# Splitting the last output pass of a two-layer diffusion step into two passes of 160 tokens

## The chip, the cores and the metric

The kernel runs on one core of one Trainium2 chip. The metric is the device time of one launch in microseconds (us). Five engines work side by side, each with its own instruction queue: TensorE (PE; its weight loads are listed apart as PEld), VectorE (DVE), ScalarE (ACT), GpSimd (POOL) and SyncE (SP), which starts the transfers to and from the device memory.

## The reference, cut to what matters

The program is one inference step of a two-layer backbone over 128 context tokens and 512 latent tokens, 640 in all, with 1024 features each. Each layer runs FFN, token mixer, FFN; after each of these six stages (numbered 0 to 5) comes a residual sum and a LayerNorm. The change lies in the last one, stage 5:

```python
def layer_norm(x, g, b):
    xf = x.astype(jnp.float32)
    mu = xf.mean(-1, keepdims=True)
    var = jnp.square(xf - mu).mean(-1, keepdims=True)
    return ((xf - mu) * lax.rsqrt(var + LN_EPS) * g + b).astype(x.dtype)

def swiglu(h, w_in, w_out):
    g, u = jnp.split(h @ w_in, 2, axis=-1)
    return (jax.nn.silu(g) * u) @ w_out
...
    x = layer_norm(ALPHA * x + 0.5 * g3 * swiglu(modulate(x, sh3, sc3), ffn_w_in_i[1], ffn_w_out_i[1]),
                   ln_g_i[2], ln_b_i[2])
```

The hidden width of the FFN is 2816. Everything is computed in float32.

## The kernel before

Features lie on the 128 partitions, tokens along the columns: `x` holds eight feature tiles (`dt` 0 to 7) of 640 tokens. The tokens are cut in two halves of 320 (`c` 0 and 1, `CSL`). A product of float32 numbers is made of three products of rounded parts (high times high, high times low, low times high); each is one matmul with a 128x128 weight tile that is loaded just for it. One such product of one hidden block, in `product`, is therefore three loads and three matmuls (lines 527, 528 and 529).

The 22 hidden blocks of the FFN come in four groups (`GROUPS`). For each group the hidden part is computed, and then the output products of that group are added to `x`. In the last group, of five blocks, one output tile is 15 matmuls (five blocks by three). `do_out(dt, c)` makes one output tile: it multiplies into one bank of PSUM and calls `residual`, in which DVE scales the bank by the gate, adds it to `x` (line 353), and GpSimd sums tiles 0 to 6 of `x` for the mean (line 357). All eight tiles of `c` = 0 run first, then all eight of `c` = 1. All weights of this last group stay in ten pairs of weight tiles, so that both halves use the same ones.

`norm_steps` is the LayerNorm of one half, a generator that is stepped by `tick` between the matmuls of other work:

- `mu`: two float32 products that give the mean in every partition (lines 401 and 403), copied by ACT to `mus` (line 405)
- `x - mu`: five tiles on DVE, three on GpSimd (line 411), squares on ACT (line 413)
- `va`: sums of the squares, with weights of only 32 columns (line 420)
- `rq`, `rx`: root on ACT (line 425), reciprocal on DVE (line 426), spread by a mask (line 428)
- `rs`: one product that copies the reciprocal root to every partition (line 432)
- `x * rs` on DVE (line 436), then, in stage 5, scale and shift on ACT (line 445) and one transfer of the tile to `y` from SP (line 447)

The LayerNorm of `c` = 0 is stepped between the output products of `c` = 1. The LayerNorm of `c` = 1 follows when all products are done; in stage 5 nothing is left that could run beside it. The program is written in this order, and a scheduler that walks through it fixes the order on each engine; after that each engine works strictly in its order.

Of the kernel before, what the change touches and what calls it, by code (L numbers as in the profile page):

```python
# [12 lines left out]
F32 = mybir.dt.float32  # L13
F32R = mybir.dt.float32r
AF = mybir.ActivationFunctionType
ALU = mybir.AluOpType
# [3 lines left out]
P = 128  # L20
D = 1024
KD = D // P
CTX = 128
LAT = 512
T = CTX + LAT
CH = T // 2
# [20 lines left out]
TICK_OUT = (1, 3, 4, 5)  # L47
TICK_IN = (1, 3, 4, 6)
# [26 lines left out]
XPOOL = ((), ())  # L75
XDVE = (tuple(range(8)), (2, 5))
MPOOL = (2, 5, 7)
LAG = 2
T1, T2, T4 = (0, 1), (2, 3), (4, 5)
GTYPE_P = (0, 1, 1, 0)  # L80
# [4 lines left out]
def kernel(  # L85
# [5 lines left out]
    te, act, dve, pool, sp = nc.tensor, nc.scalar, nc.vector, nc.gpsimd, nc.sync  # L91
# [16 lines left out]
    sm = ctx.enter_context(tc.tile_pool(name="sm", bufs=2))  # L108
# [4 lines left out]
    def tmp(name, cols=T, parts=P, dt=F32):  # L113
        t = tp.tile([P, UW], F32, tag="t", name=name)
        return t[:parts, :cols]
# [9 lines left out]
    mean_w = const.tile([P, P], F32, name="mean_w")  # L125
    dve.memset(mean_w, 1.0 / D)
    qmask = const.tile([P, 4], F32, name="qmask")
# [184 lines left out]
    x = res.tile([P, KD, T], F32, name="x")  # L312
# [20 lines left out]
        for _ in range(2 * n):  # L333
            fill_step()

    CSL = (slice(0, CH), slice(CH, T))
    SEG = (((slice(0, CTX), 1), (slice(CTX, CH), 0)), ((slice(CH, T), 0),))

    def gemm(ps, wh, wl, rows, cols, kh, kl):
        n = len(rows)  # L340
# [5 lines left out]
                tick()  # L346

    s1t = [res.tile([P, CH], F32, name=f"s1_{c}") for c in range(2)]

    def residual(ps, dt, c, st, nsum=0):  # L350
        for sl, z in SEG[c]:
# [41 lines left out]
        warm = sm.tile([P, 1], F32, tag="warm", name="warm")  # L393
        act.activation(warm, src[:, 0:1], AF.Sqrt, bias=eps_t, scale=0.0)

    QC = CH // 4

    def norm_steps(c, st, bank, nsum):
        sl = CSL[c]
        mu = bank(f"mu{st}_{c}")[:, :CH]  # L400
        pin(te.matmul(mu, mean_w, s1t[c], start=True, stop=(nsum == KD)))
        for dt in range(nsum, KD):
            te.matmul(mu, mean_w, x[:, dt, sl], start=False, stop=(dt == KD - 1))
        mus = tmp(f"mus{st}_{c}", CH)
        act.copy(mus, mu)
        va = None
        for half in range(2):
            sqs = []
            for dt in range(4 * half, 4 * half + 4):
                eng = pool if dt in MPOOL else dve  # L410
                eng.tensor_tensor(x[:, dt, sl], x[:, dt, sl], mus if eng is pool else mu, ALU.subtract)
                sq = tmp(f"sq{st}_{c}_{dt}", CH)
                act.activation(sq, x[:, dt, sl], AF.Square)
                sqs.append(sq)
            yield
            if va is None:
                va = bank(f"va{st}_{c}")[:, :QC]
            for i, sq in enumerate(sqs):
                for q in range(4):
                    ins = te.matmul(va[32 * q:32 * q + 32], mean_w[:, 0:32], sq[:, q * QC:(q + 1) * QC],  # L420
                                    start=(half == 0 and i == 0), stop=(half == 1 and i == 3))
                    if i == 0 and q == 0:
                        pin(ins)
        rq = sm.tile([P, QC], F32, tag="rq", name=f"rq{st}_{c}", bufs=1)
        act.activation(rq, va, AF.Sqrt, bias=eps_t)
        dve.reciprocal(rq, rq)
        rx = tmp(f"rx{st}_{c}", CH)
        dve.tensor_tensor(rx.rearrange("p (q n) -> p q n", q=4), rq.unsqueeze(1).broadcast_to([P, 4, QC]),
                          qmask.unsqueeze(2).broadcast_to([P, 4, QC]), ALU.mult)
        yield  # L430
        rs = bank(f"rs{st}_{c}")[:, :CH]
        pin(te.matmul(rs, mean_w, rx, start=True, stop=True))
        xms = []
        for dt in range(KD + (LAG if st < 5 else 0)):
            if dt < KD:
                ins = dve.tensor_tensor(x[:, dt, sl], x[:, dt, sl], rs, ALU.mult)
                if dt > LAG:
                    pin(ins)
            if st < 5:
                if dt < KD:  # L440
                    xms.append(modulate_in(dt, c, st + 1))
                if dt >= LAG:
                    modulate_out(dt - LAG, c, xms[dt - LAG])
            else:
                act.activation(x[:, dt, sl], x[:, dt, sl], AF.Identity, bias=lnb[:, st, dt:dt + 1],
                               scale=lng[:, st, dt:dt + 1])
                sp.dma_start(out=a["y"][:, dt, sl], in_=x[:, dt, sl])

    class LayerNorm:
# [3 lines left out]
        def tick(self):  # L453
            self.n += 1
            while self.ticks and self.n >= self.ticks[0]:
                self.ticks.pop(0)
                next(self.gen, None)
# [6 lines left out]
    pending = []  # L464
# [5 lines left out]
    def settle():  # L470
        while pending:
            pending.pop(0).finish()
# [81 lines left out]
    def ffn(l, j, hp, fbank, following):  # L554
        idx = 2 * l + (0 if j == 0 else 1)
        st = 3 * l + j
# [9 lines left out]
        for g0, g1 in GROUPS:  # L566
# [67 lines left out]
            last = g1 == NF  # L634
# [4 lines left out]
            def do_out(dt, c):  # L639
                while len(out_units) < -(-(nf * (dt + 1)) // 4):  # L640
                    o = len(out_units) * 512
                    n = min(1024, nf * D - o)
                    out_units.extend(uload(a["wout"][idx, :, g0 * D + o:g0 * D + o + n], n,
                                          pool if not last and len(out_units) // 2 % OPOOL else dve))
                b = fbank(f"o{idx}_{g0}_{dt}_{c}")
                product(b, out_units, nf * dt, [(hh[k][:, CSL[c]], hl[k][:, CSL[c]]) for k in range(nf)])
                residual(b, dt, c, st, nsum)

# [8 lines left out]
            for i in range(KD + skew):  # L657
                if i < KD:
                    do_out(i, 0)
                    if i < LLAST or not last:  # L660
                        for _ in range(LOUT[0]):
                            next(lanes, None)
                if i >= skew:
                    do_out(i - skew, 1)
                    if not last:
                        for _ in range(LOUT[1]):
                            next(lanes, None)
                if i == KD - 1 and last:
                    pending.append(LayerNorm(0, st, fbank, nsum, TICK_OUT))
                if i >= KD - 1 and last:  # L670
                    tick()
                while coming and i >= KD - 1 and len(out_units) - NUNIT <= ready and nf * (i - skew + 1) >= 4 * ready + 8:
                    key = coming.pop(0)
                    at["w"] = len(following) - len(coming) - 1
                    early[key] = wload(a[key[0]][key[1:]])
                    ready += 2
            if last:
                for _ in lanes:
                    pass
                assert not coming  # L680
                at["u"] = 6
                settle()
                pending.append(LayerNorm(1, st, md_bank if (st + 1) % 3 == 1 else fbank, nsum, TICK_IN))

    def project_load(name, i):
        return [u for h in range(2) for u in halves(wget((name, i, h)))]
# [1044 lines left out]
```

## Time and profile before

| | us |
|---|---|
| three runs | 2796.84, 2799.68, 2804.33 |
| median | 2799.68 |
| the profiled execution, whole | 2800.67 |
| its span in the trace | 2798.9 |
| PE busy over the span | 96% |
| granted TensorE clock, mean over the span | 0.985 of full |

The span begins with the first and ends with the last recorded instruction; the 1.8 us between it and the whole time lie outside the trace. Times of rows count from the start of the span. The stage that the change touches is the last 38.6 us of it, from 2760.28, where the first product of `c` = 1 starts, to 2798.9.

### The profile page before, as it was taken

What the parts mean: (1) busy time and instruction counts of PE and PEld (TensorE: products, weight loads), DVE (VectorE), ACT (ScalarE), POOL (GpSimd) and SP (SyncE); (2) the same over time, 40 slices, a digit from 0 to 9 for tenths busy, and PEclk for the clock granted to TensorE, in tenths of its full rate; (3) what the DMA queues carried; (4) which work ended last, traced back from release to release, by engine and by line L of the source; (5) the groups of instructions that cost most, each with busy time, mean ns of one, the idle gap of its engine ahead of it and who ended that gap; (6) DMA issues with size and microseconds to landing.
All of it is one profiled execution on the core that took longest, in us unless ns stands there. A gap on an engine that the chain in (4) does not pass through costs nothing.

```text
span 2798.9 us, 51125 instructions
## 1 busy us (share of the span) xinstructions
PE 2683.2 (96%) x19404; PEld 2558.2 (91%) x19404; DVE 2111.8 (75%) x4778; ACT 1196.1 (43%) x2572; POOL 991.4 (35%) x811
## 2 busy tenths in 40 slices
PE   7999999999999989999999999999999998999998
PEld 6898999989999688999989899998999987999997
DVE  5797888865765688888878888886777777765765
ACT  5662432444444462424346243344433336443433
POOL 4442533440000143534425354344223234543542
PEclk9999999999999999999999999999999998999999
DMA  8623324312222523243231332332423331322321
GB/s 281 236 95 98 126 91 129 114 56 90 77 74 74 191 73 128 84 129 129 84 106 63 112 128 91 121 121 67 132 84 106 101 100 35 99 76 76 98 68 54
DMA packets 111134, 293.45 MB, mean 105 GB/s; under 512 B 13823, under 2 KB 28927, under 8 KB 110760
## 3 DMA queue, kind: packets, MB, share of 16 engines
q1 hardware_dynamic: 107576, 285.80, 31.7%
q0 software_dynamic: 2304, 4.20, 0.5%
q8 instruction: 153, 2.51, 0.4%
q14 instruction: 93, 0.76, 0.1%
q10 hardware_dynamic: 1008, 0.19, 0.1%
HBM read 275.98 MB, written 14.16 MB: 104 GB/s over the span
## 4 chain that ended last, share of the span: by engine, by line
PE 67%; DVE 17%; DMA 6%; issue 4%; ACT 3%; POOL 3%; DVEq 0%; ACTq 0%; POOLq 0%; SPq 0%
PE f L527 8%; PE f L528 8%; PE f L529 8%; PE o L527 5%; PE o L528 5%; PE o L529 5%; DVE junk L247 5%; DMA mh<-in_modt 3%; DVE wl L158 3%; PE hy L343 2%; PE hy L342 2%; PE hy L344 2%; DVE xl L158 2%; PE qk L342 1%; PE qk L343 1%
## 5 line engine op out<-in xcount | busy, mean ns | idle before, releaser
L157 ACT CAST wh<-raw 128x512 fp32r<-128x512 f32 (+1 forms) x327 | 230.4, 709 | 302.5 <-PE o L528 151.9
L158 DVE TENSOR_TENSOR wl<-raw,wh 128x512 fp32r<-128x512 f32 (+1 forms) x274 | 274.6, 1003 | 70.1 <-ACT wh L157 69.3
L527 PE MATMUL f<-xh,wh 128*128 128x320 f32 x956 | 296.3, 314 | 15.7 <-DVE q L606 10.0
L528 PE MATMUL f<-xl,wh 128*128 128x320 f32 x956 | 297.5, 312 | 2.7 <-DVE xl L390 2.7
L529 PE MATMUL f<-xh,wl 128*128 128x320 f32 x956 | 294.7, 311 | 0.0
L247 DVE SCALAR_TENSOR_TENSOR junk<-mh,condw 128x256 f32<-128x256 f32 x576 | 267.1, 510 | 32.2 <-DMA mh<-in_modt 31.4
L527 PE MATMUL o<-hh,wh 128*128 128x320 f32 x840 | 261.0, 314 | 5.2 <-ACT hh L157 5.2
L528 PE MATMUL o<-hl,wh 128*128 128x320 f32 x840 | 259.1, 309 | 0.0
L529 PE MATMUL o<-hh,wl 128*128 128x320 f32 x840 | 258.1, 309 | 0.0
L353 DVE SCALAR_TENSOR_TENSOR x<-o,drv,x 128x320 f32<-128x320 f32 (+2 forms) x384 | 153.8, 434 | 105.3 <-PE o L529 104.7
L158 DVE TENSOR_TENSOR wl<-s,wh 128x512 fp32r<-128x512 f32 x187 | 170.9, 914 | 69.0 <-ACT wh L157 65.5
L157 ACT CAST wh<-s 128x512 fp32r<-128x512 f32 x187 | 115.8, 620 | 228.6 <-POOL s L594 69.3
L527 PE MATMUL f<-xh,xh 128*128 128x320 f32 x628 | 194.6, 314 | 8.1 <-DVE q L606 4.2
L593 POOL TENSOR_TENSOR s<-raw 128x512 f32<-128x512 f32 x73 | 110.7, 1516 | 256.2 <-DVE junk L247 167.3
L527 PEld LDWEIGHTS f<-xh,wh 128*128 128x128 f32 x956 | 180.0, 189 | 21.2 <-DVE q L606 12.1
L528 PE MATMUL f<-xl,xh 128*128 128x320 f32 x628 | 195.0, 311 | 0.2 <-DVE xl L390 0.2
L529 PE MATMUL f<-xh,xl 128*128 128x320 f32 x628 | 193.1, 310 | 0.0
L595 POOL TENSOR_TENSOR s<-raw,raw 128x512 f32<-128x512 f32 x73 | 106.5, 1459 | 238.6 <-DVE wl L158 150.2
L528 PEld LDWEIGHTS f<-xl,wh 128*128 128x128 f32 x956 | 180.8, 189 | 4.7 <-DVE xl L390 4.5
L527 PE MATMUL o<-hh,xh 128*128 128x320 f32 x568 | 178.2, 316 | 3.4 <-ACT hh L157 3.4
L529 PEld LDWEIGHTS f<-xh,wl 128*128 128x128 f32 x956 | 180.6, 189 | 0.0
L528 PE MATMUL o<-hl,xh 128*128 128x320 f32 x568 | 176.7, 312 | 1.2 <-DVE hl L158 1.2
(496 smaller groups left out, 8874.0 us busy)
## 6 DMA issues: line engine op xcount, KB each, us to landing
raw<-in_win SPq DMA_DIRECT2D x176, 512.0 KB, 3.6
raw<-in_wout SPq DMA_DIRECT2D x88, 512.0 KB, 4.3
mh<-in_modt SPq DMA_DIRECT2D x144, 256.0 KB, 2.9
raw<-in_modw SPq DMA_DIRECT2D x62, 512.0 KB, 4.8
raw<-in_hyin SPq DMA_DIRECT2D x24, 512.0 KB, 3.7
ksb<-kspec SPq DMA_DIRECT2D x40, 256.0 KB, 2.7
kspec<-ks SPq DMA_DIRECT2D x32, 256.0 KB, 3.2
raw<-in_wqk SPq DMA_DIRECT2D x16, 512.0 KB, 3.5
```

What stands on the lines that cost most here:

```text
L157: act.copy(pair[0], src)
L158: (eng or dve).tensor_tensor(pair[1], src, pair[0], ALU.subtract)
L247: dve.scalar_tensor_tensor(junk, raw[:, 256 * g:256 * g + 256], 1.0, condw[0][:, z], ALU.mult, ALU.mult, accum_out=acc[:, g0 + g, t, z:z + 1])
L342: te.matmul(ps, wh[:, i, cols], kh(k), start=(i == 0), stop=False)
L343: te.matmul(ps, wh[:, i, cols], kl(k), start=False, stop=False)
L344: te.matmul(ps, wl[:, i, cols], kh(k), start=False, stop=(i == n - 1))
L353: dve.scalar_tensor_tensor(x[:, dt, sl], ps[:, o], drv[:, st, 2, dt, z:z + 1], x[:, dt, sl], ALU.mult, ALU.add)
L527: te.matmul(ps, wh, kh, start=(first and i == 0), stop=False, skip_group_check=True)
L528: te.matmul(ps, wh, kl, start=False, stop=False, skip_group_check=True)
L529: te.matmul(ps, wl, kh, start=False, stop=(last and i == n - 1), skip_group_check=True)
L593: eng.tensor_tensor(s1, a21, a22, ALU.add)
L595: eng.tensor_tensor(s3, a11, a21, ALU.subtract)
```

## The change

Only stage 5 is touched. The second half (`c` = 1, 320 tokens) is cut in two quarters of 160 tokens, `c` = 2 and `c` = 3. Where the eight output tiles of `c` = 1 were made, those of `c` = 2 are made, beside the LayerNorm of `c` = 0 as before. Then the eight tiles of `c` = 3 are made with the same weights, and the LayerNorm of `c` = 2 is stepped beside them. The LayerNorm of `c` = 3 comes last. In it, three of the eight scale-and-shift steps (`dt` 1, 4 and 6) run on GpSimd and five on ACT. The number of output matmuls of the second half goes from 120 of 320 columns to 240 of 160 columns. The output is stored in 24 transfers (8 of 320 columns, 16 of 160), where there were 16 of 320. The sums for the mean of the two quarters lie in the two halves of the tile that `c` = 1 used.

```diff
+LPOOL = (1, 4, 6)
...
-    CSL = (slice(0, CH), slice(CH, T))
-    SEG = (((slice(0, CTX), 1), (slice(CTX, CH), 0)), ((slice(CH, T), 0),))
+    HALF = CH + CH // 2
+    CSL = (slice(0, CH), slice(CH, T), slice(CH, HALF), slice(HALF, T))
+    SEG = (((slice(0, CTX), 1), (slice(CTX, CH), 0)),) + tuple(((sl, 0),) for sl in CSL[1:])
+    WIDTH = tuple(sl.stop - sl.start for sl in CSL)
...
+    s1t += [s1t[1][:, 0:CH // 2], s1t[1][:, CH // 2:CH]]
...
-        mu = bank(f"mu{st}_{c}")[:, :CH]
+        n, qc = WIDTH[c], WIDTH[c] // 4
+        mu = bank(f"mu{st}_{c}")[:, :n]
...
-                act.activation(x[:, dt, sl], x[:, dt, sl], AF.Identity, bias=lnb[:, st, dt:dt + 1],
-                               scale=lng[:, st, dt:dt + 1])
+                if c == 3 and dt in LPOOL:
+                    pool.tensor_scalar(x[:, dt, sl], x[:, dt, sl], lng[:, st, dt:dt + 1], lnb[:, st, dt:dt + 1],
+                                       ALU.mult, ALU.add)
+                else:
+                    act.activation(x[:, dt, sl], x[:, dt, sl], AF.Identity, bias=lnb[:, st, dt:dt + 1],
+                                   scale=lng[:, st, dt:dt + 1])
                 sp.dma_start(out=a["y"][:, dt, sl], in_=x[:, dt, sl])
...
-                b = fbank(f"o{idx}_{g0}_{dt}_{c}")
+                b = fbank(f"o{idx}_{g0}_{dt}_{c}")[:, :WIDTH[c]]
...
-                    do_out(i - skew, 1)
+                    do_out(i - skew, 2 if last and st == 5 else 1)
...
+                if st == 5:
+                    pending.append(LayerNorm(2, st, fbank, nsum, TICK_OUT))
+                    for dt in range(KD):
+                        do_out(dt, 3)
+                        tick()
                 settle()
-                pending.append(LayerNorm(1, st, md_bank if (st + 1) % 3 == 1 else fbank, nsum, TICK_IN))
+                pending.append(LayerNorm(3 if st == 5 else 1, st, md_bank if (st + 1) % 3 == 1 else fbank, nsum, TICK_IN))
```

Up to the first product of the second half, every engine has the same instructions in the same order in both kernels. Three places behind that point follow, as the order of the engines prints them; `o_17_4_1` is output tile 4 of half 1 in the group that starts with block 17, and a number behind it only tells buffers apart.

On DVE, around the reciprocal of the LayerNorm of `c` = 0, before:

```order
L353 SCALAR_TENSOR_TENSOR x<-o_17_3_1_30270,drv,x 128x320
L426 RECIPROCAL rq_0_30304<-rq_0_30304 128x80
L428 TENSOR_TENSOR rx_0_30307<-rq_0_30304,qmask 128x320
L353 SCALAR_TENSOR_TENSOR x<-o_17_4_1_30309,drv,x 128x320
L436 TENSOR_TENSOR x<-x,rs_0_30327 128x320 x8
```

and after:

```order
L357 SCALAR_TENSOR_TENSOR x<-o_17_3_2_30270,drv,x 128x160
L429 RECIPROCAL rq_0_30304<-rq_0_30304 128x80
L357 SCALAR_TENSOR_TENSOR x<-o_17_4_2_30309,drv,x 128x160
L431 TENSOR_TENSOR rx_0_30307<-rq_0_30304,qmask 128x320
L439 TENSOR_TENSOR x<-x,rs_0_30327 128x320 x8
```

The residual step of output tile 4 now stands ahead of `rx`; before it stood behind it.

On PE, at the end of output tile 4 of the second half, after (before, the same rows stand here with 320 columns):

```order
L534 MATMUL o_17_4_2_30309<-hh_21_29343,wh_106 128x160
L535 MATMUL o_17_4_2_30309<-hl_21_29348,wh_106 128x160
L536 MATMUL o_17_4_2_30309<-hh_21_29343,wl_107 128x160
L435 MATMUL rs_0_30327<-rx_0_30307,mean_w 128x320
L534 MATMUL o_17_5_2_30353<-hh_17_29339,wh_106 128x160
L535 MATMUL o_17_5_2_30353<-hl_17_29344,wh_106 128x160
```

The product `rs`, which reads `rx`, stands between tiles 4 and 5 in both kernels.

On GpSimd, the end of the program, after:

```order
L414 TENSOR_TENSOR x<-x,mus_0_30191 128x320 x3
L361 TENSOR_TENSOR s_1_115<-x 128x160
L361 TENSOR_TENSOR s_1_115<-x,s_1_115 128x160 x5
L414 TENSOR_TENSOR x<-x,mus_2_30426 128x160 x3
L361 TENSOR_TENSOR s_1_115<-x 128x160
L361 TENSOR_TENSOR s_1_115<-x,s_1_115 128x160 x5
L414 TENSOR_TENSOR x<-x,mus_3_30644 128x160 x3
L449 TENSOR_SCALAR x<-x,lng,lnb 128x160 x3
```

The sums and subtractions of the second half stand twice, at half the width, and the three scale-and-shift steps are the last of the engine.

## Rows read from the trace of the kernel before

**Rows 1.** PE in order of time: start us, us, engine, line, operation, output<-inputs, weights, moving shape

```profile
2760.28 0.31 PE L527 MATMUL o<-hh,xh 128*128 128x320 f32 x1
...
2760.72 0.31 PE L527 MATMUL o<-hh,xh 128*128 128x320 f32 x1
...
2781.62 0.70 PE L401 MATMUL mu<-s,mean_w 128*128 128x320 f32 x2
```

**Rows 2.** The chain that ended last, behind the last product: start us, us, what

```profile
2781.82 0.56 DVE x L353
...
2782.43 0.82 PE mu L403 x2
...
2783.32 0.43 ACT mus L405
...
2783.85 0.50 DVE x L411
...
2784.37 0.94 ACT sq L413 x2
...
2788.07 0.34 ACT rq L425
...
2788.43 0.66 DVE rq L426
...
2789.19 0.50 DVE rx L428
...
2789.74 1.45 PE rs L432 x2
...
2791.74 3.38 ACT x L445 x6
...
2795.66 0.54 ACT x L445
```

**Rows 3.** Weight loads (PEld) in order of time, columns as in rows 1

```profile
644.30 0.19 PEld L343 LDWEIGHTS qk<-xl,wh 128*128 128x128 f32 x1
644.41 0.19 PEld L344 LDWEIGHTS qk<-xh,wl 128*128 128x128 f32 x1
...
1980.51 0.97 PEld L1420 LDWEIGHTS ivc<-ib,yc 128*128 128x128 f32 x8
```

**Rows 4.** Short matmuls of the attention scores on PE, columns as in rows 1

```profile
637.85 0.27 PE L853 MATMUL sc<-qk1h,qk0l 64*128 64x192 f32 x2
637.96 0.28 PE L853 MATMUL sc<-qk1l,qk0h 64*128 64x192 f32 x2
```

**Rows 5.** Reciprocal and mask of the LayerNorm of c = 0: DVE and PE, by time

```profile
2772.18 0.41 PE L527 MATMUL o<-hh,wh 128*128 128x320 f32 x1
...
2772.68 0.65 DVE L426 RECIPROCAL rq<-rq 128x80 f32<-128x80 f32 x1 [0.53 <-ACT rq L425]
...
2773.36 0.49 DVE L428 TENSOR_TENSOR rx<-rq,qmask 128x320 f32<-128x320 f32 x1
```

**Rows 6.** Groups by shape: line, engine, shapes, count | busy us, mean ns | idle before

```profile
L353 DVE SCALAR_TENSOR_TENSOR x<-o,drv,x 128x128 f32<-128x128 f32 x8 | 2.8, 348 | 8.1 <-PE o L529 8.1
...
L157 ACT CAST wh<-raw 128x512 fp32r<-128x512 f32 x257 | 157.0, 617 | 208.8 <-PE o L528 147.5 <-PE f L528 34.5 <-DMA raw<-in_wout 8.1
...
L157 ACT CAST wh<-raw 128x1024 fp32r<-128x1024 f32 x70 | 73.3, 1048 | 93.6 <-PE hy L343 38.5 <-PE qk L343 21.6 <-DMA raw<-in_hyout 14.2
```

**Rows 7.** GpSimd: subtraction of the mean, and scale and shift (min/median/max ns)

```profile
L411 POOL TENSOR_TENSOR x<-x,mus 128x320 f32<-128x320 f32 x6 | 5.1, 876 | 8.1 <-ACT mus L405 8.1
...
L477 POOL TENSOR_SCALAR x<-x,lng,lnb x80: 600/668/4672, 585.5 to 2383.3; 128x320 f32<-128x320 f32 x80
```

**Rows 8.** SP's queue where four transfers are started behind one another

```profile
2311.61 1.72 SPq L494 DMA_DIRECT2D condw<-in_condw  x4
```

**Rows 9.** Busy us by stretch (count): PE, PEld, DVE, ACT, POOL, clock, DMA share, GB/s

```profile
2770.00:2780.00 10.00, 10.00 (x103) 9.41 (x92) 6.35 (x14) 5.06 (x10) 2.63 (x3) 1.00 0.23 84
...
2790.00:2799.00 9.00, 1.17 (x2) 0.24 (x2) 3.27 (x8) 4.46 (x8) 0.00 (x0) 0.50 0.40 146
```

More of the change, by code (lines that the diff above doesn't have):

```diff
@@ L394, in sqrt_ready @@
         act.activation(warm, src[:, 0:1], AF.Sqrt, bias=eps_t, scale=0.0)
-    QC = CH // 4
     def norm_steps(c, st, bank, nsum):
         sl = CSL[c]
-        mu = bank(f"mu{st}_{c}")[:, :CH]
+        n, qc = WIDTH[c], WIDTH[c] // 4
+        mu = bank(f"mu{st}_{c}")[:, :n]
         pin(te.matmul(mu, mean_w, s1t[c], start=True, stop=(nsum == KD)))
@@ L403, in norm_steps @@
             te.matmul(mu, mean_w, x[:, dt, sl], start=False, stop=(dt == KD - 1))
-        mus = tmp(f"mus{st}_{c}", CH)
+        mus = tmp(f"mus{st}_{c}", n)
         act.copy(mus, mu)
@@ L411, in norm_steps @@
                 eng.tensor_tensor(x[:, dt, sl], x[:, dt, sl], mus if eng is pool else mu, ALU.subtract)
-                sq = tmp(f"sq{st}_{c}_{dt}", CH)
+                sq = tmp(f"sq{st}_{c}_{dt}", n)
                 act.activation(sq, x[:, dt, sl], AF.Square)
@@ L416, in norm_steps @@
             if va is None:
-                va = bank(f"va{st}_{c}")[:, :QC]
+                va = bank(f"va{st}_{c}")[:, :qc]
             for i, sq in enumerate(sqs):
                 for q in range(4):
-                    ins = te.matmul(va[32 * q:32 * q + 32], mean_w[:, 0:32], sq[:, q * QC:(q + 1) * QC],
+                    ins = te.matmul(va[32 * q:32 * q + 32], mean_w[:, 0:32], sq[:, q * qc:(q + 1) * qc],
                                     start=(half == 0 and i == 0), stop=(half == 1 and i == 3))
@@ L423, in norm_steps @@
                         pin(ins)
-        rq = sm.tile([P, QC], F32, tag="rq", name=f"rq{st}_{c}", bufs=1)
+        rq = sm.tile([P, qc], F32, tag="rq", name=f"rq{st}_{c}", bufs=1)
         act.activation(rq, va, AF.Sqrt, bias=eps_t)
         dve.reciprocal(rq, rq)
-        rx = tmp(f"rx{st}_{c}", CH)
-        dve.tensor_tensor(rx.rearrange("p (q n) -> p q n", q=4), rq.unsqueeze(1).broadcast_to([P, 4, QC]),
-                          qmask.unsqueeze(2).broadcast_to([P, 4, QC]), ALU.mult)
+        rx = tmp(f"rx{st}_{c}", n)
+        dve.tensor_tensor(rx.rearrange("p (q n) -> p q n", q=4), rq.unsqueeze(1).broadcast_to([P, 4, qc]),
+                          qmask.unsqueeze(2).broadcast_to([P, 4, qc]), ALU.mult)
         yield
-        rs = bank(f"rs{st}_{c}")[:, :CH]
+        rs = bank(f"rs{st}_{c}")[:, :n]
         pin(te.matmul(rs, mean_w, rx, start=True, stop=True))
```

## The prediction

> **What bounds the kernel now.** I read the share of each engine first: PE is busy for 96% of the span, so up to the last product a change counts by what it adds to PE or makes PE wait, and behind the last product by the chain that runs alone. The order of the engines is the same in both kernels up to the first product of the second half, so all before 2760.28 stays, and 38.6 us are left to look at, in two pieces.
>
> The first is PE from 2760.28 to 2781.62 [rows 1], 21.34 us. Three matmuls of 320 columns start in 0.44 us there, a pace of 0.147; 120 of them make 17.6. The other 3.74 us are the LayerNorm of c = 0, products and waits, stepped in between. The second is the chain of waits from 2781.62 to the end at 2798.9, 17.28 us [rows 2]: last residual step, mean, copy, first subtraction, eight squares on ACT, root, reciprocal, mask, product rs, multiplication, scale and shift, transfer. Each step waits for the one before it and nothing runs beside them. Their cost goes with the columns, and this is what half the width can shorten. In the first piece, more matmuls can only cost.
>
> **The change, part one: 240 products in place of 120.** The columns in all stay the same (240 times 160 is 120 times 320), but there are 240 weight loads where there were 120. At a pace in proportion to the columns a matmul of 160 would take 0.073 and nothing would be lost. The question is whether a 128x128 load can come that often. Three places show loads with little to cover them. Single loads that each last 0.19 start 0.11 apart (644.30 and 644.41), and eight with short matmuls last 0.97 together, so (0.97 - 0.19) / 7 = 0.111 from one to the next [rows 3]. Score matmuls of 192 columns, which in proportion would need 0.088, start 0.11 apart as well (637.85 and 637.96) [rows 4]. In none of the three do loads start closer than 0.11, however short the matmul, so I take 0.11 for the pace: 240 x 0.110 = 26.4, against 17.6: **+8.8**. The bounds are 0.073 (nothing) and 0.128 (load and matmul partly by turns, below).
>
> **Part two: the LayerNorm of c = 2 now stands between products of c = 3.** It is new on PE. The LayerNorm of c = 0 cost 3.74 for 320 columns; half of that is 1.87, the whole 3.74 the upper end. Its loads don't shrink with the columns, and its waits only partly: **+2.1**, nearer to the half since its matmuls have half the columns.
>
> **Part three: a wait for rs of c = 0.** Before, DVE does the reciprocal, then the mask rx, then the residual step of tile 4; after, that residual step stands ahead of rx. It needs the end of tile 4, and PE's next instruction, rs, needs rx. So rs waits for all products of tile 4, then for the residual step and for rx, and behind rs all products of tiles 5 to 7 are queued on PE. In the trace of before PE took up tile 4 at 2772.18, and the reciprocal ended at 2773.33, 1.15 later [rows 5]. After, the ten matmuls of tile 4 that stand behind the last sum of squares take 10 x 0.11 = 1.1, their result is out some 0.2 later, the residual step takes 0.37 (a step of 128 columns takes 0.348 [rows 6], one of 320 takes 0.56 [rows 2]) and rx 0.49 [rows 5]. With the gaps between them rs starts about 2.3 after PE took up the tile, where PE is free at 1.1 to 1.2: 1.05 of waiting, and a load of 0.11 that nothing hides, **+1.15**. If the scheduler's order is met by other times it is 0; with a later root, 1.4.
>
> PE so comes to its last product 8.8 + 2.1 + 1.15 = 12.05 later than before, at about 2793.7.
>
> **Part four: the end with 160 columns.** Step by step, from [rows 2]: residual 0.56 to 0.37 (-0.18). Mean, PE 0.82 to 0.55 (-0.27). Its copy 0.43 to 0.30 (-0.13). First subtraction 0.50 to 0.33 (-0.17). Squares: an ACT operation goes with 0.84 ns a column, from (1048 - 617) / 512 of two shapes [rows 6], so 160 columns fewer save 0.134 each, eight of them -1.07. The root has 40 in place of 80 columns, -0.04. Reciprocal 0.66 to 0.39, in proportion but for a fixed part, -0.27 (bounds 0 and -0.33). Mask 0.50 to 0.34, -0.16. The product rs 1.45 to 0.92, -0.53: it is slow since the granted clock is at 0.50 by then [rows 9], and stays so. First multiplication -0.17. That is 2.99 in all.
>
> Then scale, shift and store. Before, from the first to the end of the last, 2791.74 to 2796.20, 4.46 us. After, DVE still multiplies eight tiles, at 0.33 each, and two engines share the scaling, so neither ACT nor DVE sets the pace any longer. SP does: it starts eight transfers one behind another, and four in a row took 1.72, or 0.43 each [rows 8]. So the first scaled tile (0.51 with its wait) and seven transfers of 0.43: 3.5, **-0.95**. Ends: if SP were faster, DVE's multiplications would set 3.05 (-1.4). GpSimd's three scalings can cost up to the other side: the same operation on 320 columns took 0.60, 0.67 in the median and up to 4.67 us [rows 7]. In that tail GpSimd has nothing else, and DVE's second input is rs in PSUM, so I take the short end. GpSimd's three subtractions (0.88 each at 320 columns [rows 7]) end beside ACT's squares and cost nothing, as long as eight squares of 0.34 outlast three of 0.5. The transfers behind the last scaling stay at 2.7 us. The end is shorter by 2.99 + 0.95 = **3.94**. The transfers of c = 2, eight more on SP, run under the products of c = 3 (the DMA share is 0.23 in such a stretch, [rows 9]), at no cost; without that cover they would be 8 x 0.43.
>
> **Sum.** 12.05 - 3.94 = +8.1. The profiled execution took 2800.67, so 2808.8; it lay 1.0 above the median of its runs, so on the median 2807.8, 0.29% more. With p for the pace of the narrow products the result is 2799.68 + 240 p - 18.3. Its own range, with the bounds of the parts together where they can be (p 0.105 to 0.112, c = 2 1.87 to 3.74, wait 0 to 1.4, tail -4.4 to -2.9), is 2804.5 to 2811.
>
> **Rivals.** *Load and matmul partly take turns.* The loads with short matmuls [rows 3] could be read as 0.055 for the load and the rest for the matmul; with 160 columns it would be 0.055 + 0.073 = 0.128. Then 30.7 for the products, +12.4, 2812.1: slower. It decides from p = 0.111 on. Against it: 64 columns and 192 columns have the same 0.11 [rows 3, 4]. *Loads are hidden more than that.* In the rows at 0.11 each load still lasts 0.19, so neighbouring loads overlap, and beside longer matmuls they may overlap more. Halfway between 0.073 and 0.110, at 0.092, the products take 22.0, and the sum is +3.7: 2803.4. What speaks for it is that no row has 160 columns; against it, that 192 columns do not go below 0.11 [rows 4]. The Trainium skill speaks for this one too: "TensorE: Matmul & The Clock Gate", section "Back-to-back issue gap", gives about 81 ns for each load and matmul of 128 columns in a long stream, from which the estimate would be 19.4 us for the products and 2800.8 in all; the 192-column row does not agree with it. *Pace in proportion to the columns*, 0.073: the products cost nothing, and 2.1 + 1.15 - 3.94 leaves -0.7, 2799.0: not slower. Only here does the shorter end win; it decides below p = 0.076. *The clock falls.* If narrow products let TensorE drop to its lower level (0.50, 1.2 GHz), p doubles to 0.22, +35, 2834. Against it: the clock is 1.00 while products run and 0.50 only where PE did 1.17 us of work in 9 [rows 9], and after the change PE has more to do up to the last product, not less. *The change doesn't do what it says in the end:* the three scalings on GpSimd are of the long kind [rows 7] and set the end, +3: 2810.8.
>
> **How the numbers follow.** Forecast 0.70, turns 0.09, more hidden 0.10, in proportion 0.06, clock 0.03, GpSimd 0.02. About 0.3%, 8.4 us, is what a measurement of this kernel can tell from no change, so the bounds are 2791.3 and 2808.1. The forecast itself lies 0.3 us within: 0.38 of its 0.70 goes to same, 0.32 to slower. Slower: 0.32 + 0.09 + 0.03 + 0.02 = 0.46. Faster: 0.02, the lower tail of the proportional case, with a tail that saves more than counted. Same: 0.38 + 0.10 + 0.04 = 0.52. The range takes in the turns case above, to 2812.5, and the more-hidden one below, most of the way to the proportional one, 2800.5.
>
> **What would show it.** In the profile of the changed kernel the products of 160 columns should start 0.11 apart with PEld busy nearly throughout; PE should wait about 1.1 us at rs of c = 0 for rx; the last product should end its load phase at about 2793.7; and from there 13.3 us should be left, with SP's transfers 0.43 apart as the last row of waits. The prediction is wrong at its largest term if those starts are 0.073 to 0.09 or 0.128 apart, or the granted clock is below 1.00 while they run; at part three if PE goes from tile 4 to rs without waiting; at part four if the last transfer waits for GpSimd or if the span behind the last product is not between 12.5 and 14.5.

## The result, and the profile after

| | kernel before | changed kernel |
|---|---|---|
| median of 20 runs, us | 2797.39 | 2807.53 |
| lowest and highest, us | 2791.56, 2804.33 | 2800.74, 2831.17 |
| ratio of the changed kernel to the one before | | 1.0052, 95% interval 1.0034 to 1.007 |
| profiled execution, whole; span; granted clock | 2800.67; 2798.9; 0.985 | 2810.38; 2808.6; 0.985 |

The change makes the kernel slower, by more than 0.3%. The 20 times of the changed kernel are of two kinds: 14 lie between 2800.7 and 2811.3 at a mean granted clock of 0.984 or more (their median is 2806.15, 8.8 above the kernel before), and six between 2822.2 and 2831.2 at 0.977 to 0.981. The 20 times of the kernel before have no second kind. The profiled execution is of the first kind, and is read first.

What comes ahead of the first product of the second half is the same in both kernels, yet that product starts at times from 2750.4 to 2765.4 in the profiled executions of this study. So stretches from that product on are compared, not spans. Products of the second half in the changed kernel, PE in order of time (start us, us, engine, line, operation, output<-inputs, weights, moving shape):

```profile
2760.82 0.31 PE L536 MATMUL o<-hh,xl 128*128 128x320 f32 x1
2760.97 0.24 PE L534 MATMUL o<-hh,xh 128*128 128x160 f32 x1
...
2761.38 0.27 PE L535 MATMUL o<-hl,xh 128*128 128x160 f32 x1
...
2762.50 0.27 PE L536 MATMUL o<-hh,xl 128*128 128x160 f32 x1
2762.61 0.74 PE L404 MATMUL mu<-s,mean_w 128*128 128x320 f32 x2
```

From 2761.38 to 2762.50 ten matmuls start, 0.112 apart, where the rows of 320 columns were 0.147 apart [rows 1]. Half the columns took three quarters of the time. By stretch (length; busy us and count of PE, PEld, DVE, ACT, POOL; granted clock; DMA share; GB/s), up to the mean of the last LayerNorm and from there:

```profile
2760.97:2795.03 34.06, 33.18 (x382) 31.33 (x381) 16.14 (x47) 14.64 (x36) 10.42 (x18) 1.00 0.14 50
2795.03:2808.60 13.57, 3.91 (x72) 2.38 (x71) 4.29 (x16) 4.79 (x15) 2.90 (x6) 0.64 0.24 73
```

The first was 21.34 and is 34.06: +12.72. The second was 17.28 and is 13.57: -3.71. Together +9.0, and 0.7 of the 9.7 between the spans lies ahead of both. PE is busy for 33.18 of 34.06; the missing 0.88 is one wait, at rs of c = 0 (a row's last part in brackets is the engine's idle time before it and what ended that):

```profile
2771.99 0.65 DVE L429 RECIPROCAL rq<-rq 128x80 f32<-128x80 f32 x1 [1.55 <-ACT rq L428]
...
2772.56 0.28 PE L536 MATMUL o<-hh,wl 128*128 128x160 f32 x1
2772.88 0.38 DVE L357 SCALAR_TENSOR_TENSOR x<-o,drv,x 128x160 f32<-128x160 f32 x1 [0.23 <-PE o L536]
2773.18 0.48 DVE L431 TENSOR_TENSOR rx<-rq,qmask 128x320 f32<-128x320 f32 x1
...
2773.72 0.81 PE L435 MATMUL rs<-rx,mean_w 128*128 128x320 f32 x2 [0.88 <-DVE rx L431]
```

The reciprocal is done at 2772.64, but DVE then waits for the last matmul of tile 4 and does its residual step; only then comes rx. PE starts its last matmul at 2772.56 and the next one 1.16 later. Before, rx followed the reciprocal at once [rows 5].

The end of the changed kernel, the chain that ended last (start us, us, what), and the last eight stores on SP's queue:

```profile
2795.23 0.39 DVE x L357
2795.67 0.55 PE mu L406 x2
2796.30 0.30 ACT mus L408
2796.70 0.33 DVE x L414
2797.05 0.35 ACT sq L416
...
2799.52 0.30 ACT rq L428
2799.85 0.41 DVE rq L429
2800.35 0.34 DVE rx L431
2800.73 0.91 PE rs L435 x2
2801.67 0.33 DVE x L439
2802.03 1.80 ACT x L452 x4
```

```profile
2802.57 3.65 SPq L454 DMA_DIRECT2D out_y<-x  x8
```

Each step takes 0.6 to 0.7 of its row in [rows 2], except the root (0.30 against 0.34) and the scalings (0.45 each against 0.56). ACT and GpSimd share the scalings and have ended them by 2804.24, but SP, which starts one store each 0.47, is at its stores until 2806.22.

### The profile page after: what moved, and what is told of

Read it like the earlier page. It is cut to its first block, busy times and chain, and to the rows that moved or that the text cites. A ratio compares the mean times of both kernels' runs of the same rounds, so it can differ in the third digit from the quotient of the medians.

```text
span 2808.6 us, 51582 instructions
## 1 busy us (share of the span) xinstructions
PE 2693.5 (96%) x19594; PEld 2570.4 (92%) x19594; DVE 2111.8 (75%) x4801; ACT 1198.3 (43%) x2587; POOL 992.9 (35%) x823
## 4 chain that ended last, share of the span: by engine, by line
PE 68%; DVE 17%; DMA 5%; issue 4%; ACT 3%; POOL 3%; DVEq 0%; ACTq 0%; POOLq 0%; SPq 0%
PE f L534 8%; PE f L535 8%; PE f L536 8%; PE o L534 5%; PE o L535 5%; PE o L536 5%; DVE junk L248 5%; DMA mh<-in_modt 3%; DVE wl L159 3%; PE hy L346 2%; PE hy L345 2%; PE hy L347 2%; DVE xl L159 2%; PE qk L345 1%; PE qk L346 1%
## 5 line engine op out<-in xcount | busy, mean ns | idle before, releaser
L534 PE MATMUL o<-hh,wh 128*128 128x320 f32 (+1 forms) x864 | 267.1, 312 | 5.3 <-ACT hh L158 5.3
L535 PE MATMUL o<-hl,wh 128*128 128x320 f32 (+1 forms) x864 | 265.2, 308 | 0.0
L536 PE MATMUL o<-hh,wl 128*128 128x320 f32 (+1 forms) x864 | 264.3, 307 | 0.0
L357 DVE SCALAR_TENSOR_TENSOR x<-o,drv,x 128x192 f32<-128x192 f32 (+3 forms) x392 | 155.3, 428 | 108.1 <-PE o L536 107.7
L534 PE MATMUL o<-hh,xh 128*128 128x320 f32 (+1 forms) x584 | 181.5, 313 | 3.3 <-ACT hh L158 3.3
L535 PE MATMUL o<-hl,xh 128*128 128x320 f32 (+1 forms) x584 | 180.1, 310 | 1.2 <-DVE hl L159 1.2
```

Source lines behind the costliest of these rows:

```text
L357: dve.scalar_tensor_tensor(x[:, dt, sl], ps[:, o], drv[:, st, 2, dt, z:z + 1], x[:, dt, sl], ALU.mult, ALU.add)
L534: te.matmul(ps, wh, kh, start=(first and i == 0), stop=False, skip_group_check=True)
L535: te.matmul(ps, wh, kl, start=False, stop=False, skip_group_check=True)
L536: te.matmul(ps, wl, kh, start=False, stop=(last and i == n - 1), skip_group_check=True)
```

## Experiments

Each kernel is timed beside the kernel before. Where a verdict needs less than 3 us, it goes by two lengths from the trace: the stretch from the first product of the second half to the mean of the last LayerNorm (21.34 before, 34.06 changed), and the end from there (17.28 and 13.58; the row above ends 0.01 early).

**The pace of narrow products alone.** Edit to the kernel before:

```diff
-                product(b, out_units, nf * dt, [(hh[k][:, CSL[c]], hl[k][:, CSL[c]]) for k in range(nf)])
+                cuts = 2 if last and st == 5 and c == 1 else 1
+                for h in range(cuts):
+                    o, m = h * CH // cuts, CH // cuts
+                    cs = slice(CSL[c].start + o, CSL[c].start + o + m)
+                    product(b[:, o:o + m], out_units, nf * dt, [(hh[k][:, cs], hl[k][:, cs]) for k in range(nf)])
```

> The kernel before, with one thing changed: each output tile of c = 1 in the last group of stage 5 is multiplied in two column halves, so 240 matmuls of 160 columns with 240 loads stand where 120 of 320 stood; residual steps, LayerNorm and stores keep their 320 columns and the order of DVE stays that of before. Theory (a 128x128 load is not ready sooner than 0.111 after the one before): the products take 240 x 0.111 = 26.6 in place of 17.6, the stretch from the first product of c = 1 to the mean of c = 1 goes from 21.3 to 30.3, the end behind it stays 17.3; +9.0 in all, and no wait at rs of c = 0. Rival (the loss of the change lies in its LayerNorm and waits, the products cost less than counted): the stretch stays under 27. On the slower executions of the changed kernel (some of its runs took 20 us more at a mean clock of 0.977): if narrow products make the clock fall in some executions, this kernel has such runs too; if the two passes or the stores do it, it has none.

Measured: five runs, 2806.6 to 2811.0, ratio 1.0033 (1.002 to 1.0046); stretch 30.08, +8.74; end 17.35. PE, first and last narrow products:

```profile
2758.76 0.24 PE L527 MATMUL o<-hh,xh 128*128 128x160 f32 x1
...
2788.73 0.27 PE L529 MATMUL o<-hh,xl 128*128 128x160 f32 x1
2788.84 0.74 PE L401 MATMUL mu<-s,mean_w 128*128 128x320 f32 x2
```

The largest term of the loss is the products by themselves, with nothing done to the LayerNorm. No execution of the second kind.

**Four pieces of 80 columns.** The same edit with `cuts = 4`.

> As the run with two column halves, but in four pieces of 80 columns: 480 matmuls and loads. Theory (floor of 0.111 whatever the width): 480 x 0.111 = 53.3 in place of 17.6, +35.7. Rival (each matmul has a fixed part and a part by the column, fitted to 0.147 at 320 and 0.111 at 160: 0.075 + 0.000225 a column): 0.093 at 80 columns, 480 x 0.093 = 44.6, +27. Rival (load and matmul by turns): 0.092 to 0.10. If narrow products make the clock fall in some executions, runs with a lower mean clock are longer by more than 20 here, since 53 us of products stand there.

Measured: four runs, 2875.9 to 2890.3, ratio 1.0291 (1.0273 to 1.0308), more than twice what any of the theories gave. At first the pace is the one expected, PE in order of time:

```profile
2765.42 0.28 PE L528 MATMUL o<-hl,xh 128*128 128x80 f32 x1
...
2768.54 0.28 PE L529 MATMUL o<-hh,xl 128*128 128x80 f32 x1
2768.66 0.31 PE L527 MATMUL o<-hh,xh 128*128 128x80 f32 x1
2768.77 0.42 PE L528 MATMUL o<-hl,xh 128*128 128x80 f32 x1
2768.99 0.41 PE L529 MATMUL o<-hh,xl 128*128 128x80 f32 x1
```

28 matmuls start in the 3.12 us to 2768.54, 0.111 apart, as with 160 columns, and the rivals' 0.09 to 0.10 are out. It is no floor of every matmul: those of the sums of squares, whose weights have 32 columns, come far closer (24 in 0.62, a row of the changed kernel), so it goes with the 128x128 load.

```profile
2769.12 0.62 PE L423 MATMUL va<-sq,mean_w 128*32 128x80 f32 x24
```

In the kernel with four pieces that pace did not last: from 2768.77 on they come 0.213 apart. The windows of that kernel (columns as above) say why:

```profile
2765.05:2768.50 3.45, 3.45 (x34) 3.45 (x32) 0.68 (x2) 0.00 (x0) 0.00 (x0) 1.00 0.00 0
...
2769.00:2772.00 3.00, 3.00 (x16) 3.00 (x16) 0.00 (x0) 0.00 (x0) 0.00 (x0) 0.50 0.00 0
...
2800.00:2869.00 69.00, 69.00 (x373) 68.00 (x373) 7.17 (x15) 5.62 (x11) 4.32 (x5) 0.50 0.05 20
```

The granted clock fell from 1.00 to 0.50, from 2.4 to 1.2 GHz, while PE and its loads were busy for the whole of the row before. It did not rise again while the 80-column products lasted: the stretch is 104.8 us.

**All scalings on ACT.** Edit to the changed kernel:

```diff
-LPOOL = (1, 4, 6)
+LPOOL = ()
```

> The changed kernel with all eight scale-and-shift steps of c = 3 on ACT, none on GpSimd. In the changed kernel the stores of c = 3 are started 0.475 apart by SP and the last start (2805.84) comes 1.6 after the last scaling has ended. Theory (SP sets the end): ACT needs 8 x 0.45 = 3.6 from 2802.03, the last scaling ends near 2805.6 and its store starts at the same 2805.8 or 0.1 later; 0 to +0.2 us. Rival (the three steps on GpSimd carry the gain of the end): +1.4, since ACT then has eight in place of five.

Measured: six runs, two at 2803.4 and 2809.3, four at 2822.0 to 2830.0. The eight scalings end at 2825.08, 0.41 after one another, and the last store starts at 2825.49; SP's eight stores take 3.65 as in the changed kernel:

```profile
2821.68 3.40 ACT L452 ACTIVATE x<-x,lnb,lng 128x160 f32<-128x160 f32 x8 [2.22 <-DVE x L439]
2822.22 3.65 SPq L454 DMA_DIRECT2D out_y<-x  x8
```

From the first to the last start it is 3.27 in both: the three steps on GpSimd are worth nothing while SP starts all stores. This profiled execution is one of the second kind. No profile of a long execution of the changed kernel itself is kept, but this one has the same products and the same wait, and shows what such an execution looks like:

```profile
2767.00:2770.00 3.00, 3.00 (x44) 2.71 (x46) 1.92 (x6) 2.52 (x7) 2.79 (x5) 1.00 0.00 0
2770.00:2773.00 3.00, 3.00 (x70) 2.48 (x58) 0.76 (x2) 0.80 (x2) 0.53 (x1) 1.00 0.02 5
2773.00:2774.50 1.50, 0.63 (x6) 0.47 (x5) 1.06 (x3) 0.00 (x0) 0.46 (x1) 1.00 0.00 0
2774.50:2776.00 1.50, 1.50 (x6) 1.13 (x7) 0.41 (x2) 0.00 (x0) 0.18 (x1) 0.54 0.00 0
...
2779.00:2814.00 35.00, 35.00 (x218) 34.30 (x218) 7.45 (x25) 7.77 (x21) 5.69 (x11) 0.50 0.13 45
```

The clock falls right behind the wait at rs of c = 0 (the 0.63 busy of 1.50), and stays at 0.50 through all the narrow products that follow. The stretch takes 52.67 in place of 34.06. The experiments that follow, up to the two queues, are about that wait.

**rs one tile later.** Edit to the changed kernel:

```diff
-                    pending.append(LayerNorm(0, st, fbank, nsum, TICK_OUT))
+                    pending.append(LayerNorm(0, st, fbank, nsum, (1, 3, 4, 6) if st == 5 else TICK_OUT))
```

> The changed kernel with the product rs of the LayerNorm of c = 0 (stage 5) stepped one output tile later, behind tile 5 of c = 2. Theory (the wait of PE at rs comes from the residual step that stands ahead of rx on DVE): the wait of 1.15 (2772.56 to 2773.72 less the load) goes, PE comes to the mean of c = 3 about 1.1 us earlier, the end is unchanged: -1.1. Rival (the wait turns into another one, at the residual steps behind eight multiplications on DVE or at the mean of c = 2): 0.

Measured: twelve runs, median 2805.32, ratio 1.0024 (1.0011 to 1.0037); stretch 32.65, -1.41; end 13.50. PE is never idle in the stretch:

```profile
2750.41:2783.07 32.66, 32.66 (x383) 31.10 (x381) 16.15 (x47) 14.53 (x36) 10.44 (x18) 1.00 0.15 52
```

The wait goes and no other takes its place. From the last product of tile 4 to the product behind rs it was 1.56 in the changed kernel (2772.56 to 2774.12), and where rs doesn't wait that distance is 0.45, so the wait itself cost 1.11. The other 0.3 of the 1.41 comes behind rs, where the sums of squares of the LayerNorm of c = 2 stand in two blocks of 32 matmuls here and in three blocks (8, 24 and 32) in the changed kernel. None of the twelve runs lies above 2817.4; two are at 2814.5 and 2817.4, at clocks of 0.984 and 0.981. No profile of these two is kept, and the mean clock over the whole span doesn't tell the kinds apart alone: an execution of the kernel before had 0.981 too, at 2805.2.

**The wait with wide products, and with narrow ones.** Edit to the kernel before (first run) and to the kernel with two column halves (second run): the residual step of tile 4 is kept ahead of rx, as in the changed kernel.

```diff
+        if (c, st) == (0, 5):
+            yield
         rx = tmp(f"rx{st}_{c}", CH)
-        dve.tensor_tensor(rx...)
+        ins = dve.tensor_tensor(rx...)
+        if (c, st) == (0, 5):
+            pin(ins)
...
+            if (st, c, dt, nsum > 0) == (5, 1, 4, True):
+                pin(ins)
...
-                    pending.append(LayerNorm(0, st, fbank, nsum, TICK_OUT))
+                    pending.append(LayerNorm(0, st, fbank, nsum, (1, 3, 4, 5, 5) if st == 5 else TICK_OUT))
```

> The kernel before with its 120 products of 320 columns, but with the order on DVE that the change brought: the residual step of output tile 4 ahead of rx, so that PE waits at rs of c = 0. Theory for the wait: tile 4 ends at about 2774.4, its result 0.25 later, residual 0.55, rx 0.49, so rs starts 1.2 later than before; +1.2. Theory for the clock (it falls only where the products are narrow): no execution more than 10 above the others, mean clock 0.98 or more in all. Rival (a wait of about 1 us on PE at this place is enough to make the clock fall): some executions 15 to 25 above the others at a lower mean clock.

Measured: eleven runs, 2794.6 to 2804.1, ratio 1.0012 (1.0001 to 1.0024); stretch 22.64, +1.30; end 17.28. No run of a second kind. The row of rs:

```profile
2772.03 0.81 PE L438 MATMUL rs<-rx,mean_w 128*128 128x320 f32 x2 [1.04 <-DVE rx L432]
```

> The run with two column halves (240 products of 160 columns, LayerNorm and stores as before) with the same order on DVE as the other run of this call: the residual step of tile 4 ahead of rx, so that PE waits about 1.3 at rs of c = 0. In executions at full clock +8.7 + 1.3 = +10.0 against the kernel before. Theory for the clock (narrow products bring TensorE near its limit, and a wait among them makes it fall in some executions): some executions 15 to 25 longer at a mean clock of 0.975 to 0.981, where the five of the run without the wait had none. Rival (the wait has no part in it; the LayerNorm of c = 2 between narrow products makes it fall): none, as in the run without the wait.

Measured: five runs, 2808.2 to 2809.8, ratio 1.005 (1.0035 to 1.0065); stretch 31.42, 1.34 more than without the wait. PE waited 1.14 at rs here, and the clock stayed at 1.00:

```profile
2773.00:2776.00 3.00, 3.00 (x54) 2.80 (x53) 1.20 (x2) 0.33 (x1) 0.87 (x1) 1.00 0.00 0
2776.00:2779.00 3.00, 1.86 (x17) 1.66 (x15) 0.95 (x2) 0.00 (x0) 0.81 (x1) 1.00 0.00 0
2779.00:2789.20 10.20, 10.20 (x92) 10.12 (x91) 4.38 (x10) 4.48 (x8) 1.90 (x3) 1.00 0.36 130
```

So the size of the wait is settled, 1.3 us in both of these kernels. The theory for the clock expected some long executions among the five, and none came. Five are too few to call it wrong: at the rate of the kernels with the change's products and the wait (13 of 32, below) five in a row without a fall come by chance about once in 13 times. What the changed kernel has beside narrow products and a wait is that its tiles take half the time, so the LayerNorm of c = 0 and its wait stand closer together (between the last sum of squares and rs stand ten matmuls there, thirty here), and that the LayerNorm of c = 2 comes behind it.

**Without the LayerNorm of c = 2 between products.** Edit to the changed kernel; the second run has the edit of "rs one tile later" as well.

```diff
-                    pending.append(LayerNorm(2, st, fbank, nsum, TICK_OUT))
+                    pending.append(LayerNorm(2, st, fbank, nsum, (99,)))
```

> The changed kernel with the LayerNorm of c = 2 taken out of the products of c = 3: it runs behind all products, ahead of that of c = 3. What stands between the products of c = 2 (LayerNorm of c = 0, the wait at rs) is as in the changed kernel. At full clock: the products of c = 3 take 13.3, about 2.3 less than with the LayerNorm between them, and the end is longer by the LayerNorm of c = 2, some 9 to 11: 2814 to 2817. Theory (the clock falls at the wait for rs of c = 0, which stands 3 us behind the short matmuls of that LayerNorm, as the row of the run without GpSimd's scalings showed): executions 15 to 30 longer at a mean clock near 0.98 as in the changed kernel, 3 to 5 of 10. Rival (the LayerNorm of c = 2 between the products is needed): none.

Measured: six runs; two at 2811.0 and 2816.1 with a clock of 0.985, four at 2823.9 to 2833.9 with 0.976 to 0.982. The profiled one is of the second kind, and its clock falls where it fell above, behind the wait for rs of c = 0:

```profile
2768.00:2771.00 3.00, 3.00 (x65) 2.59 (x64) 0.66 (x2) 1.34 (x4) 1.56 (x4) 1.00 0.02 5
2771.00:2774.00 3.00, 2.12 (x22) 1.77 (x22) 1.44 (x3) 0.33 (x1) 0.70 (x2) 0.98 0.00 0
2774.00:2777.00 3.00, 3.00 (x13) 2.61 (x13) 1.95 (x5) 1.43 (x3) 0.02 (x1) 0.50 0.00 0
```

The profiled execution of the changed kernel, which is of the first kind, has the same matmuls and the same wait in these three microseconds, and its clock stayed at 1.00 up to the last product:

```profile
2771.00:2774.00 3.00, 2.12 (x22) 1.77 (x22) 1.44 (x3) 0.33 (x1) 0.70 (x2) 1.00 0.00 0
```

So the wait does not bring the fall in every execution.

> The other run of this call with the LayerNorm of c = 2 at the end, and rs of c = 0 one output tile later, so that PE doesn't wait there. Theory (the wait makes the clock fall): no execution with a mean clock under 0.983, 1.4 less than the other run's executions at full clock. Rival (narrow products and the short matmuls of the LayerNorm of c = 0 are enough without a wait): as many longer executions as in the other run.

Measured: six runs, 2808.3 to 2816.7, clocks 0.982 to 0.986; stretch 36.63. Of the numbers expected, the bound of 0.983 was broken by one run. Four of six long executions with the wait and none above 2816.7 without it: the LayerNorm of c = 2 between the products is not needed for the fall, and the wait is part of it. Six runs each are few, but they agree with the two pairs above: the kernels with the change's products and the wait (the changed one, ACT only, two queues) had 13 of 32 executions above 2821, the one without the wait 0 of 12.

**Two queues for the stores.** Edit to the changed kernel:

```diff
-                sp.dma_start(out=a["y"][:, dt, sl], in_=x[:, dt, sl])
+                out_q = act if c == 3 and dt in (3, 5, 7) else sp
+                out_q.dma_start(out=a["y"][:, dt, sl], in_=x[:, dt, sl])
```

> The changed kernel with three of the eight stores of c = 3 (tiles 3, 5, 7) started by ACT in place of SP. Theory (SP's pitch of 0.475 sets the end): SP starts five, ACT three; the last scaling ends about 2.2 + 3 x 0.1 to 0.4 after the first, the last store starts 0.5 to 1.0 earlier than in the changed kernel, so the end from the mean of c = 3 goes from 13.6 to 12.6 to 13.1. Rival (ACT pays for the stores what SP saves, its scalings are delayed by 0.4 for each store): 13.6 or more. Executions with a fallen clock as in the changed kernel, since its products are the same.

Measured: stretch 34.06, end 12.64, which is 0.93 shorter:

```profile
2806.99 2.31 SPq L455 DMA_DIRECT2D out_y<-x  x5
...
2807.87 0.87 ACTq L455 DMA_DIRECT2D out_y<-x  x2
2808.79 0.52 ACT L452 ACTIVATE x<-x,lnb,lng 128x160 f32<-128x160 f32 x1 [0.54 <-ACT x L452]
2809.34 0.34 ACTq L455 DMA_DIRECT2D out_y<-x  x1
```

SP did set the end. The rival is half right: ACT starts two stores ahead of its last scaling, which so comes 0.54 later, and its store is the last. The six runs are 2812.2 to 2824.0, three of them at a clock of 0.983 or more (2812 to 2814); these three are longer than most of the changed kernel's. In the profiled one, 2813.9, that lies ahead of the stretch, which began at 2765.39, not 2760.97; why, and whether it is so in the other two, is open.

**A cut that avoids the floor.** Edit to the kernel before, its core (`c` 2 and 3 stand for the 400 and the 240 tokens); scalings of tiles 1, 4 and 6 go to GpSimd and stores of tiles 3, 5 and 7 to ACT in the last LayerNorm:

```diff
+    W0 = 400
+    CSL = (slice(0, CH), slice(CH, T), slice(0, W0), slice(W0, T))
...
+                if last and st == 5:
+                    c += 2
...
-                    pending.append(LayerNorm(0, st, fbank, nsum, TICK_OUT))
+                    pending.append(LayerNorm(2 if st == 5 else 0, st, fbank, nsum, (1, 3, 4, 6) if st == 5 else TICK_OUT))
```

> Another cut: in the last group of stage 5 the tokens are cut 400 and 240 in place of 320 and 320, so that the products stay 120 and 120 and only the last LayerNorm gets narrower; rs of the first LayerNorm is stepped one tile later; scalings of tiles 1, 4, 6 on GpSimd and stores of tiles 3, 5, 7 started by ACT in the last LayerNorm. Theory (a product costs the larger of 0.111 and 0.147 x columns / 320): 400 columns 0.183, 240 columns 0.111; 120 x 0.183 + 120 x 0.111 = 35.3 where 35.2 stood, no loss. The end has 80 columns fewer: half of the 3.0 of the steps and 0.5 to 1.0 of the stores, from 17.3 to 15.0 to 15.8. The LayerNorm between the products is 80 columns wider: +0.5. In all -1.0 to -1.8. Rival (the cut moves waits into the products, as the change did): 0 to +2. [...]

Measured: eleven runs, ratio 1.0006 (0.9995 to 1.0016): the same. No run of a second kind. The products cost what the theory says (240 columns 0.112 apart), and the end is 14.06, 3.2 less. From the first product of c = 0 to the end it is 59.78, where the kernel before has 59.72. The rival won. The first pass is 4.27 longer (25.38 against 21.11, its 80 columns more), the second only 1.0 shorter (20.34), where the products alone would give 120 x (0.147 - 0.112) = 4.2: the rest went into a LayerNorm of 400 columns and into a new wait at the mean of the second half:

```profile
2781.89 0.67 PE L407 MATMUL mu<-s,mean_w 128*128 128x240 f32 x2 [1.90 <-POOL s L361]
```

DVE has eight multiplications of 400 columns ahead of the last residual steps, so GpSimd's sum for the mean ends late.

**The end alone, and a mild cut.** Edit to the kernel before, on top of GpSimd's scalings and the two queues; the second run has `W0 = 352` as well (rs at its old place):

```diff
-                act.activation(sq, x[:, dt, sl], AF.Square)
+                if (c, st) == (1, 5) and dt in (4, 6):
+                    dve.tensor_tensor(sq, x[:, dt, sl], x[:, dt, sl], ALU.mult)
+                else:
+                    act.activation(sq, x[:, dt, sl], AF.Square)
```

> The kernel before with its products untouched, and only the end of the last LayerNorm changed: squares of tiles 4 and 6 on DVE, scale and shift of tiles 1, 4, 6 on GpSimd, stores of tiles 3, 5, 7 started by ACT. Theory: ACT's eight squares (2784.37 to 2788.07 before) become six, the last sum comes 0.7 to 0.9 earlier; the eight scalings go from a pitch of 0.545 (ACT) to 0.50 (DVE's multiplications), 0.3 to 0.5 less: the end from the mean of c = 1 goes from 17.28 to 15.8 to 16.3, -1.0 to -1.5 in all, less than a comparison of times can tell. Rival (DVE's squares come behind its five subtractions and end after ACT's): 0 to -0.5.

Measured: end 16.42, -0.86, a little less than expected; eleven runs, ratio 0.9999 (0.9986 to 1.0011).

> The last group of stage 5 cut 352 and 288 in place of 320 and 320 (no wait added at the mean as with 400 and 240, since the first LayerNorm is only 10% wider), with the end of the last LayerNorm as in the other run of this call that changes only the end. Theory: products 120 x (0.161 + 0.132) = 35.2, as before; LayerNorm between the products +0.4; the end 32 columns narrower, a fifth of the 3.0 that 160 columns gave, on top of the other run's gain: 1.8 to 2.5 less than before from the first product of c = 0 to the end (59.7). Rival (a wait at rs or at the mean takes it back): within 0.5 of the other run.

Measured: 58.45 from the first product of c = 0 to the end, 1.27 less than before, short of the 1.8 to 2.5 of the theory. It is 0.4 less than with the end alone, which is what the rival said; eleven runs, ratio 1.0004 (0.9993 to 1.0014). Both shorten the stage in the trace, neither by as much as a timing can tell. No version here is shown to beat the kernel before.

## Why the prediction was right, and where not

The forecast was +8.1 and 2807.8; the executions at full clock give +8.8 (2806.15 against 2797.39), and the median of all is 2807.53. The agreement of that median with the forecast is in part luck: the forecast was counted from the median of three runs, 2799.68, which lies 2.3 above that of twenty, and six executions of another kind, of which below, lift the measured median by 1.4.

- **Products.** 0.110 a matmul, +8.8. Measured 0.112, which makes 26.9 for the 240 of them, +9.3; the stretch of the kernel that changes nothing else grew by 8.74. The 0.5 between the two is put down to the LayerNorm of c = 0, whose sums of squares stand in two blocks there and in three before; no run shows that by itself. Taking the pace from the closest loads of the old trace [rows 3] instead of from the columns was the step that decided. With 80 columns the pace is still 0.111, so it is a floor of the load and no slope. The rivals that gave 0.092, 0.128 and 0.073 are out. The Trainium skill, "TensorE: Matmul & The Clock Gate", section "Back-to-back issue gap", gives about 81 ns for 128 columns. The traces here do not agree: 0.11 for the transposes of 128 columns (row below), and 0.111 even at 80 columns.
- **LayerNorm of c = 2.** +2.1 was taken. What is left of 34.06 behind 240 x 0.112 = 26.9, the 3.74 of c = 0 and the wait of 1.11 at rs is 2.3. The two runs with rs one tile later say the same: from the first product of c = 2 to the last of c = 3 it is 32.65 with the LayerNorm of c = 2 in between and 30.67 without, 2.0 less, and the 0.3 behind rs comes on top in the changed kernel.
- **The wait at rs.** +1.15 from the order on DVE and rows of before. Measured 1.11 (1.56 where 0.45 stands without a wait); taking it away gave -1.41, of which 0.3 is not the wait, and putting it into the kernel before +1.30.
- **The end.** -3.94 was forecast, -3.71 measured. Up to the first scaling it went from 10.12 to 7.00 (2795.03 to 2802.03), 3.12 less where 2.99 was forecast. From there it went from 7.16 to 6.58, 0.58 less where 0.95 was. That term was off by the pace of the stores: 0.43 between SP's starts [rows 8], measured 0.47. That GpSimd's part would matter less than SP was right; with all stores on SP it matters not at all.
- **The clock: the step that failed.** The rival "the clock falls" got 0.03 and 2834. It happened in 6 of 20 executions, at 2822 to 2831. One reason that they stay under 2834: in both profiles that show the fall with 160 columns it comes at the wait, 13 us into the stretch. From there on the pace nearly doubles (0.213), as the rival had it. The reasons held against it do not hold. The row with the clock at 0.50 where PE had little work [rows 9] shows a fall, but not that busy rows are safe from one: with 80 columns the clock fell in a row where PE and PEld were busy throughout. That PE has more to do up to the last product did not keep the clock up either. The wait of part three was costed at 1.15, its own length; in 13 of 32 executions it went along with a fall that cost some 15 to 25 us.
- **The chances.** 0.52 was put on a result within 0.3% and 0.46 on slower. It is slower: the part at full clock lies at 0.31%, on the bound, as the forecast did, and the executions at the low clock bring the ratio to 1.0052.

One place was misread, without harm to the forecast. A row of [rows 4] is a pair of matmuls (x2) with weights of 64 rows each, whose loads start together, so 0.11 is the distance of pairs there and not that of two 128x128 loads, and the row speaks neither against the rival of loads hidden more nor against the 81 ns. What it was meant to show stands in another row of the old trace: four transposes of 128 columns last 0.60 together, and a single one 0.27, so they start (0.60 - 0.27) / 3 = 0.11 apart.

```profile
643.97 0.60 PE L882 MATMUL tp<-ident,S 128*128 128x128 f32 x4
```

What stays open: which neighbours a wait must have for the clock to fall. A wait of 1.1 us between 160-column products went along with no fall in the kernel with two column halves (0 of 5 executions, too few to rule one out), and with a fall in part of the executions of the changed one and its relatives. There the short matmuls of the LayerNorm, the wait and the narrow products stand closer together. That this nearness is the cause was not tried by itself.

## What to carry to other kernels

Before a matmul is cut in two, look in the trace for the closest spacing of two loads of the same size: where the half would run faster than that, the cut costs the difference for each matmul. Here the end that the cut made 3.7 shorter did not pay for the 12.7 that the products and their waits took more. Look also at what the cut does to the order on the engines that feed PE, since a wait of 1 us costs more than its length where it goes along with a fall of the clock, and time the change often enough that a second kind of execution shows.

## What the runs showed that was not expected

- The granted clock can fall while PE and its weight loads are busy without a gap: with 80-column products from 1.00 to 0.50 in the profiled execution. The times of all four (2876 to 2890) fit that, where the floor alone at 1.00 would give about 2835 (the 2799 of the kernel before and 35.7). It stayed there to the end of the products.
- At 0.50 the matmuls of 160 and of 80 columns come equally 0.213 apart, near twice 0.111 (fourteen of 160 columns start between 2779.11 and 2781.88 in the profile of the kernel with all scalings on ACT): the floor of the load goes with the clock.
- SP starts stores of a 160-column tile 0.475 apart, nearer together than ACT's scalings of 320 columns come (0.545), and further apart than those of 160 (0.41): by halving the tiles the limit of the end passed from ACT to SP.
